# Modulation rows, the last squares and the attention unit's order in a two-layer hybrid block

## The chip, the cores and the metric

The kernel runs on one core of one Trainium2 chip. The metric is the device time of one execution in microseconds (us). Five engines work in parallel and wait for each other by semaphores: TensorE (PE) multiplies, VectorE (DVE) and ScalarE (ACT) do elementwise work, GpSimd (POOL) helps a little, SyncE (SP) issues the transfers.

## What is computed

Two layers on 128 context tokens and 512 latent tokens, 1024 wide. Layer 0 mixes with a pooling branch and a gated convolution, layer 1 with grouped attention; each has a gated feed-forward part, and a shift, scale and gate that come from a conditioning vector.

```python
def modulate(x, g, shift, scale):
    return rms_norm(x, g) * (1 + scale) + shift
...
        sh1, sc1, g1, sh2, sc2, g2 = ada_params(c, w_ada[l], b_ada[l])
        h = modulate(x, norm_g[l, 0], sh1, sc1)
        if l % 2 == 0:
            y = even_mixer(h, w_in_even[i], pool_w[i], pool_scale[i], conv_w[i], conv_b[i], w_out_even[i])
        else:
            q, k, v = qkv_proj(h, w_qkv[i], q_gain[i], k_gain[i])
...
            y = blocked_attention(q, k_all, v_all) @ w_o[i]
        x = x + g1 * y
        h = modulate(x, norm_g[l, 1], sh2, sc2)
        x = x + g2 * swiglu(h, w_ffn_in[l], w_ffn_out[l])
    y_sample = rms_norm(x, final_g)
```

## The kernel before

**Layout.** All 640 tokens lie along the free axis; features lie on the 128 partitions in 8 blocks. Each fp32 operand is split into a high part and a remainder (`pair`, L143: ACT copies, DVE subtracts), and each product is three matmuls, high by high, high by low and low by high (`block_mm`, L286). A weight block of 128 output features is 48 matmuls of about 148 ns, 7.1 us in all.

**Stages.** In the order of the trace: a startup written out by hand (to 53 us); the mixer's input projection "pi", 13 blocks besides the first three (to 155 us); its output projection "po" (to 212 us); the feed-forward part of layer 0, whose 22 hidden blocks are worked in three passes of 8, 8 and 6, each with a first product "fi" and a second product "fo" (to 655 us); the q, k and v projection "pq" and attention (to 870 us); the rest of attention's output projection "wb"; layer 1's feed-forward part; and the final norm. Most of "fi" (line L648) is a fast scheme in `fast_blocks` with seven half-size products per unit, p1 to p7.

**Order.** The program is traced once, in the order of the Python code. Outside the startup a list scheduler at compile time takes for every engine the ready instruction that was traced first, and it judges readiness by a model of its own. So the traced order is a priority and not the final order. After that each engine runs its queue strictly in order.

**Modulation rows.** The shift, scale and gate vectors of a layer have 48 blocks of 128 numbers. A "row" in this text is what gives one block: a weight tile of 128 x 1024, loaded by one transfer of 512 KB, multiplied by two conditioning vectors and summed on DVE (`AdaDve.run`, L362, multiply-and-sum at L377). In layer 0's mixer it takes two DVE instructions of 1024 columns; later, where the scratch tile is a PSUM bank of 512 columns, four. `ada.run(n)` puts n rows at a place in the traced order, and `self.load()` at its end asks for a later row. `PI_ROWS` (L39) gives the rows ahead of each "pi" block, L1081 those of "po", and `each` and `fast_each` (L1099, L1100) those of the feed-forward part: `each` by block of a second product, `fast_each` by unit n and product p of the fast scheme. `EARLY` (L37) rows must be done when "po" ends.

**Pooling.** `mixer_in` (L1044) gives the first four blocks to `pool_branch` (L936), which adds shifted copies on DVE (L949) and later scales and splits (`pool_mid`, L955) and multiplies by a small matrix (`pool_end`, L972). A block's result leaves PSUM in `scaled_main` (L536, instruction L538 on DVE) and `scaled` (L543 on ACT); the three PSUM tiles of two banks go round, so the third next tile needs this.

**Between "po" and "fi".** `updater` (L580) adds a block to x (L513, L527), squares it, prepares it for the next product (`prep`, L490 and L492) and, after the last block, copies the shift into two extra columns (`prep_shift`, L505 and L506), which the first "fi" block reads.

**Attention.** 34 units: one head by 128 queries, and two units for the context queries. `scores` multiplies q and k into PSUM tile 0; `peak` and `exps` are the softmax; `weights` normalises; `turn` transposes into PSUM tile 1; `keep` splits the result into a "pt" tile, of which there is one for each part (the pool has one buffer) and which holds two units; `values` multiplies by v and reads that tile; `store` splits the outcome. In the loop unit u's scores go with the turn of unit u-1 and, for every second unit, the values of unit u-2. `fills` are quarters or eighths of projection blocks ("pieces" of "pq" and "wa", 6 matmuls or 12), which give PE work between.

**The end.** The last two blocks of the last second product are done in two spans of 384 and 256 columns (`last1`, L1477). For each span the squares of all eight blocks are summed, on DVE for the last two (L447), and a matmul with a matrix of ones (L471, plain fp32, two passes) sums over partitions. Then come Ln, Exp and three DVE steps (L478 to L483), and the scaled output (L1491).

Of the kernel before, what the change touches and what calls it, by code (L numbers as in the profile page):

```python
# [11 lines left out]
AF = mybir.ActivationFunctionType  # L12
# [5 lines left out]
KB = D // P  # L18
# [17 lines left out]

EARLY = 28  # L37

PI_ROWS = (1, 1, 0, 0, 1, 1, 2, 1, 2, 2, 2, 1, 2)  # L39
WINDOWS = (2, 4, 8, 16)  # L40
PAD = 8
UL = PAD + CTX + PAD + LAT + PAD
# [20 lines left out]
def hybrid_step(  # L63
# [23 lines left out]
    V, S, G, PE = nc.vector, nc.scalar, nc.gpsimd, nc.tensor  # L87
# [8 lines left out]
    def ps_tile(name, at=None):  # L96

        if at is None:
            at = ps_turn[0] % ps_turn[1]
            ps_turn[0] += 1  # L100
        return psum.tile([P, 2, 512], F32, tag=f"mm{at}", bufs=1, name=name)
# [4 lines left out]
    def tmp(name):  # L106
        return tpool.tile([P, UL], F32, tag="t", name=name)

    x = pers.tile([P, KB, T], F32, name="x")
    bufA = (pers.tile([P, KB, TX], F32R, name="ah"), pers.tile([P, KB, TX], F32R, name="al"))  # L110
    bufB = (pers.tile([P, KB, TX], F32R, name="bh"), pers.tile([P, KB, TX], F32R, name="bl"))
    sm = pers.tile([P, NS], F32, name="sm")
    kc = pers.tile([P, NC], F32, name="kc")
    ones = pers.tile([P, P], F32, name="ones")
# [4 lines left out]
    rstd = pers.tile([P, T], F32, name="rstd")  # L119
# [70 lines left out]
    class Stream:  # L190
# [7 lines left out]
        eng = V  # L198
# [222 lines left out]
    class Norm:  # L421
# [24 lines left out]
            if k:  # L446
                (eng or G).tensor_tensor(out=self.acc[:, cols], in0=self.acc[:, cols], in1=sq[:, cols], op=ALU.add)  # L447

        def finish(self, span=None, spare=7, eng=None):
            rsqrt_of(self.acc, rstd, self.name, 1, span, spare, eng)  # L450

    def log_exp_tables():
        tc.keep_in_program_order(S.preload_act_table_set("natural_log_exp_and_others"))

    def rsqrt_of(acc, out, name, f, span=None, spare=None, eng=None):

        if span is None:
            a, b, cut = 0, T, halves  # L460
            ps = ps_tile(f"ms_{name}")
            ms = pmain(ps)
            to = [(ps[:, h, 0:HT], h * HT, h * HT + HT) for h in range(2)]
        else:
            a, b = span
            cut = lambda t: t
            ms = ps_small(f"ms_{name}_{a}")[:, 0 : b - a]
            to = [(ms, a, b)]
        if spare is None:
            for p, lo, hi in to:  # L470
                PE.matmul(p, ones, acc[:, lo:hi], start=True, stop=True)  # L471
        else:
            pair(bufB, acc[:, a:b], lambda t: t[:, spare, a:b], eng or V)
            for i in range(2):
                for p, lo, hi in to:
                    PE.matmul(p, onesr, bufB[i][:, spare, lo:hi], start=i == 0, stop=i == 1)
        y, ac = tmp(f"y_{name}_{a}")[:, a:b], acc[:, a:b]
        S.activation(cut(y), ms, AF.Ln, bias=epst, scale=float(f))  # L478
        S.activation(y, y, AF.Exp, scale=-0.5)
        S.activation(ac, y, AF.Square)  # L480
        V.scalar_tensor_tensor(out=cut(ac), in0=ms, scalar=EPS / f, in1=cut(ac), op0=ALU.add, op1=ALU.mult)
        V.tensor_scalar(ac, ac, -0.5 * f, 1.5, op0=ALU.mult, op1=ALU.add)
        V.tensor_tensor(out=out[:, a:b], in0=y, in1=ac, op=ALU.mult)  # L483
# [87 lines left out]
    def project(name, rhs, kn, n, done, ext=False, each=None, start=0):  # L571
        cut = HT if ext else CUT
        for i in range(start, n):
            ps = ps_tile(f"{name}_{i}")
            w = ws.next()
            if each:
                each(i)
            pipe.step(lambda: block_mm(ps, w, rhs, kn, ext=ext, cut=cut), lambda: done(i, ps))
# [192 lines left out]
    with tc.tile_pool(name="pool1", bufs=1) as p1:  # L771
# [6 lines left out]
        def ada_load(ch):  # L778
# [7 lines left out]
        ada = AdaDve(  # L786
            [(0, 4, 4)]
            + [(0, 8 * p, 8) for p in (2, 4, 3)]
            + [(0, 40 + b, 1) for b in range(8)]
            + [(1, 8 * p, 8) for p in (1, 0, 2, 4, 3)]  # L790
        )
# [28 lines left out]
        nrm = Norm("a0")  # L820
# [13 lines left out]
        acc = {ch: ada_acc(ch) for ch in (2, 3)}  # L834
# [38 lines left out]
        acc = ada_acc(0)  # L873
# [185 lines left out]
        for m in range(3):  # L1059
# [8 lines left out]
            ext=True,  # L1068
            each=lambda i: ada.run(PI_ROWS[i]),
        )  # L1070

        out_done = updater(0, 16, Norm("a1"), (bufA, 0, 1))
# [5 lines left out]
            pipe.step(lambda: block_mm(fps[m], fw[m], bufB, KB, ks=range(KB - 1), cut=CUT))  # L1078
        for m in range(2):
            pipe.step(lambda: block_mm(fps[m], fw[m], bufB, KB, ks=(KB - 1,), cut=CUT), lambda: out_done(m, fps[m]))  # L1080
        project("po", bufB, KB, KB, out_done, each=lambda i: ada.run(1), start=2)  # L1081

        assert ada.at == EARLY and not ada.raw
        early.close()
# [4 lines left out]
        with tc.tile_pool(name="pool4", bufs=1) as p4:  # L1089
            ada.home(p4, p1, 2, ps_small("junk"), silb)  # L1090
            ada.limit = len(ada.todo)
            ada.load()
            ada.load()
            more = tuple(p4.tile([P, 3 * 4 * HT], F32R, tag=t, name=t) for t in ("x0h", "x0l"))
            ffn(
                0,
                bufA,
                bufA,
                each=lambda i, gi, plain=False: ada.run(0 if plain else (1, 2, 1, 2, 2, 2, 2, 2)[i] if gi == 0 else (1, 2, 2, 2, 2, 2, 1, 0)[i]),  # L1099
                fast_each=lambda gi, n, p: ada.run(int(p == 6 and gi > 0)),  # L1100
                last=last0,
                spare=(tuple(t.rearrange("p a b -> p (a b)") for t in bufB), more),
            )
            assert ada.at == len(ada.todo)

    bufA, bufB = bufB, bufA


    with tc.tile_pool(name="pool2", bufs=1) as p2:
# [274 lines left out]
        units = []  # L1384
# [30 lines left out]
        with ExitStack():  # L1415
            for u, unit in enumerate(units):
                pipe.now += 1
                for f in posts:
                    f()
                posts = []  # L1420
                unit.scores()
                last = units[u - 2] if u > 1 and units[u - 2].values else None
                if last:
                    last.values()
                if u:
                    units[u - 1].turn()
                unit.peak()
                unit.exps()
                if u:
                    units[u - 1].keep()  # L1430
                unit.weights()
                spent += W_UNIT + (W_VALUES if last else 0)
                while fills and not posts and spent + W_PIECE / 2 <= work * (u + 1) / len(units):
                    posts = [f for f in (fills.pop(0)(),) if f]
                    spent += W_PIECE
                if last:
                    last.store()
                pipe.run_due()
# [24 lines left out]
        out_done = updater(1, 16, Norm("b1"), (bufA, 1, 1))  # L1463
# [13 lines left out]
    def last1(kn):  # L1477
        nrm = Norm("fin")

        def gain(k, cols=slice(0, T)):  # L1480
            S.activation(x[:, k, cols], x[:, k, cols], AF.Copy, scale=sm[:, S_FG + k : S_FG + k + 1])

        def whole(k, ps):
            residual(ps, k, 1, 40)
            nrm.add(k)
            gain(k)

        def out(ks, cols):
            n = cols.stop - cols.start
            xs = x[:, ks, cols]  # L1490
            V.tensor_tensor(  # L1491
                out=xs, in0=xs, in1=rstd[:, None, cols].broadcast_to((P, ks.stop - ks.start, n)), op=ALU.mult
            )
            nc.sync.dma_start(yT[:, ks, cols], xs)

        project("fo1_2", bufA, kn, KB - 2, whole)
        log_exp_tables()
        w = [ws.next(), ws.next()]
        ps = [ps_tile(f"fo1_2_{m}") for m in (KB - 2, KB - 1)]
        spans = ((0, 3 * P), (3 * P, T))  # L1500
        for h, (lo, hi) in enumerate(spans):
            cols = slice(lo, hi)
            for m in range(2):
                for k in range(kn):
                    for a, b in THREE:
                        PE.matmul(
                            ps[m][:, h, 0 : hi - lo],
                            w[m][a][:, k, :],
                            bufA[b][:, k, cols],
                            start=k == 0 and a == b,  # L1510
                            stop=k == kn - 1 and a == 1,
                        )
                parts = [(c, max(a, lo), min(b, hi)) for c, a, b in SEG if a < hi and b > lo]
                update(KB - 2 + m, 1, 40, [(c, a, b, ps[m][:, h, a - lo :]) for c, a, b in parts])
                nrm.add(KB - 2 + m, V, cols)
            with tc.high_priority():
                nrm.finish((lo, hi), None)
            for m in range(2):
                gain(KB - 2 + m, cols)
            if not h:  # L1520
                out(slice(0, 4), cols)
        for h, ks in ((0, slice(4, 8)), (1, slice(0, 4)), (1, slice(4, 8))):
            out(ks, slice(*spans[h]))

    whole_b = tuple(t.rearrange("p a b -> p (a b)") for t in bufB)
    more = tuple(p3.tile([P, 3 * 4 * HT], F32R, tag=t, name=t) for t in ("xh", "xl"))
# [11 lines left out]
        last=last1,  # L1538
        spare=(whole_b, more),
        each=lambda i, gi, plain=False: gates.run(0 if plain or gi else 1),  # L1540
# [114 lines left out]
```

## Time and profile before

| | before |
|---|---|
| median of 3 runs | 1357.52 us (1357.14 to 1358.26) |
| the profiled execution's own time | 1356.08 us |
| its span, first to last instruction | 1354.3 us |
| PE busy | 1326.0 us, 98% |
| DVE busy | 1068.6 us, 79% |
| ACT busy | 637.7 us, 47% |
| mean granted TensorE clock | 0.993 |

Busy time is the time in which an engine has an instruction in hand. PE and its weight loads overlap. A wait in the profile names the engine that waited and the instruction that released it. A window row gives for a stretch of time each engine's busy time and, in brackets, its instructions, then the granted TensorE clock as a share of full speed, the share of the DMA engines and the rate.

### The profile page before, as it was taken

How to read it: one execution, taken by the hardware profiler on the slowest of the kernel's cores; microseconds unless marked ns; L12 is line 12 of the kernel's file. 1: busy time of each engine (PE TensorE's matmuls, PEld its weight loads, DVE VectorE, ACT ScalarE, POOL GpSimd, SP SyncE). 2: the span in 40 equal slices, each digit the busy share in tenths (PEclk: the TensorE clock that was granted, in tenths of full speed). 3: DMA queues.
4: the chain of work that ended last, by engine and by line, in shares of the span. 5: the costliest groups of instructions: out<-in, count | busy, mean ns of one | idle time of the engine just before them, and what ended most of it. 6: DMA issues, size and time to landing. Idle time of an engine off the chain costs nothing.

```text
span 1354.3 us, 22409 instructions
## 1 busy us (share of the span) xinstructions
PE 1326.0 (98%) x8952; PEld 1295.1 (96%) x8952; DVE 1068.6 (79%) x2025; ACT 637.7 (47%) x1159; POOL 46.3 (3%) x56
## 2 busy tenths in 40 slices
PE   8999999999999999999999999999999999999996
PEld 6899999999999999999998999999999999999995
DVE  4899897978999999899877677589876777446744
ACT  5433246753145522454666675477541355314543
POOL 0000000000000000000022221000000000000001
PEclk9999999999999999999999999999999999999998
DMA  9735522125543454334331110131134022311212
GB/s 365 286 125 171 171 94 94 63 67 176 179 141 109 146 187 151 120 137 164 133 101 48 48 48 32 51 137 60 38 137 171 32 94 76 112 63 63 78 47 78
DMA packets 36807, 155.53 MB, mean 115 GB/s; under 512 B 3936, under 2 KB 11104, under 8 KB 25952
## 3 DMA queue, kind: packets, MB, share of 16 engines
q1 hardware_dynamic: 36704, 154.12, 33.0%
q8 instruction: 70, 1.15, 0.4%
q14 instruction: 33, 0.27, 0.1%
HBM read 148.60 MB, written 2.88 MB: 112 GB/s over the span
## 4 chain that ended last, share of the span: by engine, by line
PE 82%; DVE 12%; ACT 3%; issue 2%; DMA 1%; SPq 0%; POOL 0%; DVEq 0%; ACTq 0%; POOLq 0%
PE fi L648 28%; PE fo L294 18%; PE fi L294 8%; PE pi L294 6%; PE pq L294 5%; PE po L294 4%; DVE junk L377 4%; PE wb L294 2%; PE wa L294 2%; PE o L1371 2%; PE s L1321 2%; DVE wl_fi_p L147 1%; PE t L1354 1%; DMA rawa<-wada 1%; DMA x<-xT 1%
## 5 line engine op out<-in xcount | busy, mean ns | idle before, releaser
L146 ACT ACTIVATE wh_fi_p<-raw_fi 128x512 fp32r<-128x512 f32 x252 | 154.5, 627 | 226.0 <-PE fi L648 122.3
L377 DVE CUSTOM_DVE_ANT_0 junk<-rawa,silb 128x512 f32<-128x512 f32 (+1 forms) x280 | 224.0, 800 | 7.9 <-DMA rawa<-wada 3.5
L147 DVE TENSOR_TENSOR wl_fi_p<-raw_fi,wh_fi_p 128x512 fp32r<-128x512 f32 x252 | 171.3, 687 | 65.6 <-ACT wh_fi_p L146 65.3
L146 ACT ACTIVATE wh_fo<-raw_fo 128x1024 fp32r<-128x1024 f32 (+1 forms) x48 | 47.5, 990 | 147.8 <-PE fo L294 129.5
L648 PE MATMUL fi<-bh,wl_fi_p 128*128 128x320 f32 x288 | 89.0, 309 | 0.0
L648 PE MATMUL fi<-bh,wh_fi_p 128*128 128x320 f32 x288 | 88.8, 308 | 0.0
L648 PE MATMUL fi<-ah,wl_fi_p 128*128 128x320 f32 x288 | 88.7, 308 | 0.0
L648 PE MATMUL fi<-al,wh_fi_p 128*128 128x320 f32 x288 | 88.7, 308 | 0.0
L648 PE MATMUL fi<-ah,wh_fi_p 128*128 128x320 f32 x288 | 88.4, 307 | 0.0
L648 PE MATMUL fi<-bl,wh_fi_p 128*128 128x320 f32 x288 | 88.4, 307 | 0.0
L294 PE MATMUL fo<-al,wh_fo 128*128 128x384 f32 (+1 forms) x352 | 81.0, 311 | 0.0
L294 PE MATMUL fo<-ah,wh_fo 128*128 128x384 f32 x352 | 80.8, 311 | 0.1
L294 PE MATMUL fo<-ah,wl_fo 128*128 128x384 f32 x352 | 80.5, 310 | 0.0
L294 PE MATMUL fo<-bh,wh_fo 128*128 128x384 f32 x328 | 75.2, 310 | 0.0
L294 PE MATMUL fo<-bh,wl_fo 128*128 128x384 f32 (+1 forms) x328 | 75.1, 310 | 0.0
L294 PE MATMUL fo<-bl,wh_fo 128*128 128x384 f32 x328 | 75.0, 310 | 0.0
L513 DVE SCALAR_TENSOR_TENSOR x<-fo,mod,x 128x128 f32<-128x128 f32 (+1 forms) x52 | 18.5, 359 | 70.7 <-PE fo L294 67.2
L648 PE MATMUL fi<-x0h,wh_fi_p 128*128 128x320 f32 x216 | 68.1, 319 | 0.5
L648 PE MATMUL fi<-xh,wh_fi_p 128*128 128x320 f32 x216 | 67.9, 320 | 0.5 <-ACT fi L660 0.4
L648 PE MATMUL fi<-xl,wh_fi_p 128*128 128x320 f32 x216 | 66.5, 309 | 0.0
L648 PE MATMUL fi<-xh,wl_fi_p 128*128 128x320 f32 x216 | 66.5, 309 | 0.0
L648 PE MATMUL fi<-x0h,wl_fi_p 128*128 128x320 f32 x216 | 66.4, 308 | 0.0
(376 smaller groups left out, 3774.7 us busy)
## 6 DMA issues: line engine op xcount, KB each, us to landing
raw_fi<-wfi SPq DMA_DIRECT2D x44, 1024.0 KB, 4.8
rawa<-wada SPq DMA_DIRECT2D x84, 512.0 KB, 3.4
raw_fo<-wfo SPq DMA_DIRECT2D x16, 1024.0 KB, 4.9
raw_ada<-wada SPq DMA_DIRECT2D x12, 512.0 KB, 7.3
raw_in<-win SPq DMA_DIRECT2D x6, 1024.0 KB, 5.2
raw_fo<-wfo SPq DMA_DIRECT2D x8, 768.0 KB, 4.3
raw_qkv<-wqkv SPq DMA_DIRECT2D x6, 1024.0 KB, 5.5
raw_out<-wout SPq DMA_DIRECT2D x4, 1024.0 KB, 5.9
```

Source lines behind the costliest of these rows:

```text
L146: S.activation(h, src, AF.Copy)
L147: eng.tensor_tensor(out=l, in0=src, in1=h.bitcast(F32), op=ALU.subtract)
L294: PE.matmul(ps[:, h, 0 : hi - lo], w[a][:, k, cols], rhs[b][:, k0 + k, lo:hi], start=k == 0 and a == b, stop=k == kn - 1 and a == 1,)
L377: op = V.tensor_tensor_reduce(out=self.junk, in0=raw[:, cols], in1=self.silb[:, c, cols], scale=1.0, scalar=0.0, op0=ALU.mult, op1=ALU.add ...
L513: V.scalar_tensor_tensor(out=xs, in0=got[:, 0 : b - a], scalar=mod[l][:, gate0 + m, c : c + 1], in1=xs, op0=ALU.mult, op1=ALU.add,)
L648: PE.matmul(out, w[a][:, k, :], ops.get(OPERAND[p], b)[:, k, :], start=fresh and k == 0 and a == b, stop=k == ops.kn - 1 and a == 1, skip_ ...
L1321: PE.matmul(self.ps[:, hf, 0:HT], bufB[a][:, self.h, q0 : q0 + P], kt[b][:, self.kv, hf * HT : hf * HT + HT], start=n == 0, stop=n == 2,)
L1354: PE.transpose(flat(pt)[:, s * P : s * P + P], self.pe[:, s * P : s * P + P], ident)
L1371: PE.matmul(po[:, 0 : 2 * P], vt[a][:, self.kv, s * P : s * P + P], got[b][:, s, :], start=s == 0 and n == 0, stop=s == 4 and n == 2,)
```

## The change

Four edits. (1) Modulation rows: in "pi" 14 rows in place of 16, none ahead of its first four blocks; the two others go to "po", ahead of blocks 3 and 5. (2) In layer 0's feed-forward part the first pass's second product has the row counts of the second pass's, 12 rows in place of 14 and one and none at its last two blocks; the two others go to the first pass's fast units 1 and 2, at product p6. (3) In the final norm the squares of the very last block are no longer added to the sum on DVE; they go as a second operand into the matmul with ones, which accumulates over both. (4) In attention's loop turn, keep and values come behind the pieces in the traced order, and values behind turn and keep.

```diff
-PI_ROWS = (1, 1, 0, 0, 1, 1, 2, 1, 2, 2, 2, 1, 2)
+PI_ROWS = (0, 0, 0, 0, 1, 2, 1, 2, 1, 2, 1, 2, 2)
...
-                PE.matmul(p, ones, acc[:, lo:hi], start=True, stop=True)
+                PE.matmul(p, ones, acc[:, lo:hi], start=True, stop=more is None)
+                if more is not None:
+                    PE.matmul(p, ones, more[:, lo:hi], start=False, stop=True)
...
-        project("po", bufB, KB, KB, out_done, each=lambda i: ada.run(1), start=2)
+        project("po", bufB, KB, KB, out_done, each=lambda i: ada.run(1 + (i in (3, 5))), start=2)
...
-                each=lambda i, gi, plain=False: ada.run(0 if plain else (1, 2, 1, 2, 2, 2, 2, 2)[i] if gi == 0 else (1, 2, 2, 2, 2, 2, 1, 0)[i]),
-                fast_each=lambda gi, n, p: ada.run(int(p == 6 and gi > 0)),
+                each=lambda i, gi, plain=False: ada.run(0 if plain else (1, 2, 2, 2, 2, 2, 1, 0)[i]),
+                fast_each=lambda gi, n, p: ada.run(int(p == 6 and (gi > 0 or n in (1, 2)))),
...
                 unit.scores()
                 last = units[u - 2] if u > 1 and units[u - 2].values else None
-                if last:
-                    last.values()
-                if u:
-                    units[u - 1].turn()
                 unit.peak()
                 unit.exps()
-                if u:
-                    units[u - 1].keep()
-                unit.weights()
                 spent += W_UNIT + (W_VALUES if last else 0)
                 while fills and not posts and spent + W_PIECE / 2 <= work * (u + 1) / len(units):
                     posts = [f for f in (fills.pop(0)(),) if f]
                     spent += W_PIECE
+                if u:
+                    units[u - 1].turn()
+                    units[u - 1].keep()
+                if last:
+                    last.values()
+                unit.weights()
                 if last:
                     last.store()
...
-                nrm.add(KB - 2 + m, V, cols)
+                if m:
+                    sq = tmp(f"sq_last_{h}")
+                    S.activation(sq[:, cols], x[:, KB - 1, cols], AF.Square)
+                else:
+                    nrm.add(KB - 2, V, cols)
             with tc.high_priority():
-                nrm.finish((lo, hi), None)
+                nrm.finish((lo, hi), None, more=sq)
```

More of the change, by code (lines that the diff above doesn't have):

```diff
@@ L447, in add, with finish, rsqrt_of @@
                 (eng or G).tensor_tensor(out=self.acc[:, cols], in0=self.acc[:, cols], in1=sq[:, cols], op=ALU.add)
-        def finish(self, span=None, spare=7, eng=None):
-            rsqrt_of(self.acc, rstd, self.name, 1, span, spare, eng)
+        def finish(self, span=None, spare=7, eng=None, more=None):
+            rsqrt_of(self.acc, rstd, self.name, 1, span, spare, eng, more)
     def log_exp_tables():
         tc.keep_in_program_order(S.preload_act_table_set("natural_log_exp_and_others"))
-    def rsqrt_of(acc, out, name, f, span=None, spare=None, eng=None):
+    def rsqrt_of(acc, out, name, f, span=None, spare=None, eng=None, more=None):
         if span is None:
```

## Prediction

> **What bounds the kernel now.** I read first the busy time by stage, then PE's waits, then the places of the longest waits in order of time.
>
> ```profile
> 53.00:155.00 102.00, 99.87 (x667) 99.26 (x665) 97.91 (x157) 36.66 (x62) 1.00 (x18) 0.98 0.48 163
> 155.00:212.00 57.00, 57.00 (x389) 57.00 (x388) 47.89 (x81) 20.86 (x32) 0.00 (x0) 1.00 0.35 126
> 270.00:317.00 47.00, 46.98 (x317) 46.06 (x317) 34.94 (x55) 24.79 (x48) 0.00 (x0) 1.00 0.27 90
> 317.00:382.00 65.00, 63.73 (x431) 63.49 (x430) 62.61 (x162) 12.23 (x18) 0.00 (x0) 1.00 0.51 170
> 480.00:537.00 57.00, 56.92 (x385) 56.66 (x384) 53.08 (x129) 9.54 (x13) 0.00 (x0) 1.00 0.53 182
> 710.00:870.00 160.00, 154.82 (x1116) 149.07 (x1117) 114.36 (x251) 101.38 (x212) 29.08 (x15) 1.00 0.14 44
> 1339.00:1355.00 16.00, 2.66 (x15) 1.73 (x14) 9.29 (x13) 3.77 (x10) 0.00 (x0) 0.62 0.47 164
> ```
>
> After a stretch and its length, the columns are PE, weight loads, DVE, ACT, POOL, then the granted clock. PE is the bound nearly everywhere: 57.00 of 57 in "po", 46.98 of 47 in "fi". So DVE work that moves is worth only what PE waits for it, and work on PE's own path counts in full. PE has free time in four of these rows: 2.1 us in "pi" (102.00 - 99.87), 1.3 us in the first "fo" (65.00 - 63.73), 5.2 us in attention, and the end. In the first two DVE is nearly full (97.91 of 102, 62.61 of 65). Who ended the waits:
>
> ```profile
> PE ms_fin L471 <- DVE ssq_fin L447: 2.2, 1, 2.2
> PE pi L294 <- ACT ev L543: 2.1, 1, 2.1
> PE fi L642 <- DVE x L527: 1.3, 1, 1.3
> PE t L1354 <- DVE pt_0l L147: 1.3, 3, 0.6
> PE o L1371 <- DVE pt_0l L147: 1.2, 2, 0.7
> PE t L1354 <- DVE pt_2l L147: 1.0, 1, 1.0
> PE t L1354 <- ACT pe L1240: 0.7, 1, 0.7
> PE o L1371 <- ACT pt_0h L146: 0.6, 3, 0.2
> ```
>
> Each edit aims at one of these: one wait in "pi", one ahead of "fi", the attention's five rows (4.8 us together), one at the end. The startup's waits lie ahead of all edits and stay.
>
> **Part 1a, rows out of the pooling blocks.** The wait in "pi" and what follows it:
>
> ```profile
> 78.11 0.81 DVE L538 TENSOR_TENSOR ev<-pi,rstd 128x640 f32<-128x640 f32 x1
> 79.24 0.56 PE L294 MATMUL pi<-ah,wh_in 128*128 128x320 f32 x2 [2.13 <-ACT ev L543]
> L377 DVE CUSTOM_DVE_ANT_0 junk<-rawa,silb 128x1024 f32<-128x1024 f32 x6 | 7.3, 1212 | 0.0
> 79.24 8.91 PE pi L294 x48
> 89.02 7.15 PE pi L294 x48
> 79.96:83.37 3.41, 3.41 (x15) 3.41 (x15) 3.41 (x8) 0.78 (x2) 0.00 (x0) 0.50 0.23 91
> 376.40:380.30 3.90, 2.63 (x19) 2.39 (x18) 3.83 (x13) 1.15 (x2) 0.00 (x0) 1.00 0.38 111
> ```
>
> PE needs a PSUM tile whose evacuation (L538, then L543 on ACT) stands in DVE's queue at 78.11, behind pooling and modulation. The third row groups the multiply-and-sums between 53 and 88 us: six, of which the two removed rows are four. They take DVE 4 x 1.21 = 4.8 us ahead of that evacuation, and none of the other work there waits for PE. So L538 starts near 73.3; PE followed it by 79.24 - 78.11 = 1.13, so it could go on at 74.4. It is free only at 79.24 - 2.13 = 77.1. The wait goes with 2.7 us to spare. Late next is nothing that I can find: the running count of rows in "pi" is below the old one at every block.
>
> The wait has a tail. The block behind it took 8.91 us, the next one 7.15: 1.76 us more, because the clock was granted at 0.50 for 3.41 us. The later wait of 1.3 us, last row, left it at 1.00. So the edit is worth 2.13 + 1.76 = 3.9 us. Bounds: 2.1 if the half clock comes anyway, 3.9 if not; I take 3.9, since the half clock follows at once upon this wait.
>
> [...]
>
> **Part 1b, the same rows into "po".**
>
> ```profile
> 162.10:169.20 7.10, 7.10 (x50) 7.10 (x49) 1.52 (x4) 1.14 (x2) 0.00 (x0) 1.00 0.23 74
> 169.20:204.50 35.30, 35.30 (x242) 35.30 (x241) 34.91 (x58) 14.91 (x24) 0.00 (x0) 1.00 0.25 90
> 204.50:211.60 7.10, 7.10 (x51) 7.10 (x50) 4.14 (x9) 2.66 (x5) 0.00 (x0) 1.00 0.86 295
> 208.69 0.17 DVE L506 TENSOR_TENSOR al<-mod,ah 128x16 fp32r<-128x16 f32 x1
> 211.55 0.45 PE L294 MATMUL fi<-ah,wh_fi 128*128 128x320 f32 x2
> 211.84 0.45 PE L294 MATMUL fi<-al,wh_fi 128*128 128x320 f32 x2
> 211.75 0.35 DVE L513 SCALAR_TENSOR_TENSOR x<-po,mod,x 128x128 f32<-128x128 f32 x1 [2.89 <-PE po L294]
> ```
>
> Here DVE is full: 34.91 of 35.30 us from block 2 to block 6. Two more rows are 4 x 1.22 = 4.9 us. The free time at 162 to 169 us (7.10 - 1.52) lies ahead of them and did not serve the rows of block 2 either. So DVE comes out of block 6 late by 4.9 - 0.4 = 4.5 us, and the last block has 7.10 - 4.14 = 3.0 to spare. Residuals and weight splits stand that (three PSUM tiles, weights a block ahead). The shift copies do not: the last row gives the last numbers of the shift, and "fi" reads them in its first matmuls. L506 would end at 208.69 + 0.17 + 4.5 = 213.4, where PE wants it at 211.84: 1.5 us. Bounds: 0 if the copies go ahead of the 4.1 us of other DVE work of that block (they are two instructions of 0.17), 1.5 + 1.76 = 3.3 if the wait brings the half clock too (1.3 us did not, 2.1 did). I take 1.0, nearer to the row without half clock.
>
> **Part 2, rows off the end of the first "fo".**
>
> ```profile
> L377 DVE CUSTOM_DVE_ANT_0 junk<-rawa,silb 128x512 f32<-128x512 f32 x55 | 38.2, 695 | 1.9 <-DMA rawa<-wada 1.0
> ```
>
> Modulation takes 38.2 of DVE's 62.61 us in that stage. With three rows less at the last two blocks (4 x 0.70 us each) the last residual, L527, is no longer behind them. The second pass's "fo" already has exactly these counts, and there PE has 56.92 of 57.00 us. So the 1.3 us go. The two rows that arrive in "fi" cost 2 x 4 x 0.70 = 5.6 us of DVE, which has 47.00 - 34.94 = 12.1 free. Their loads, on SP's queue, come earlier, not later. Value 1.3, between 0 (something else holds the tile) and 1.3.
>
> **Part 3, attention's order.**
>
> ```profile
> 819.43 1.78 PE wa L294 x12
> 821.22 0.90 PE s L1321 x6
> L146 ACT ACTIVATE pt_2h<-t x16: 686/704/708, 729.0 to 871.4; 128x640 fp32r<-128x640 f32 x16
> L147 DVE TENSOR_TENSOR pt_2l<-t,pt_2h x16: 808/818/826, 729.7 to 872.1; 128x640 fp32r<-128x640 f32 x16
> ```
>
> No instruction is added. PE's waits are for the softmax or for keep (0.70 + 0.82 = 1.52 us): transposes and values came to the head of the queue too early. With pieces (0.89 us for 6 matmuls, 1.78 for 12) between the scores and both of them, values get the cover of a turn more, and a turn gets a piece after its softmax. I count as gone the values' waits, 1.2 + 0.6, and the one for the softmax, 0.7: 2.5 us. The turn's waits for the free PSUM tile (1.3 + 1.0) I leave. Bounds: 4.8 (all) and, below nothing, the third rival.
>
> **Part 4, the end.**
>
> ```profile
> 1336.24 0.53 ACT L445 ACTIVATE sq_fin<-x 128x384 f32<-128x384 f32 x1 [1.95 <-DVE x L513]
> 1336.80 0.56 DVE L447 TENSOR_TENSOR ssq_fin<-ssq_fin,sq_fin 128x384 f32<-128x384 f32 x1 [0.59 <-ACT sq_fin L445]
> 1337.51 0.88 PE L471 MATMUL ms_fin<-ssq_fin,ones 128*128 128x384 f32 x2
> 1337.93 0.58 PE L1506 MATMUL fo<-bh,wh_fo 128*128 128x256 f32 x1
> 1342.38 0.34 DVE ssq_fin L447
> ```
>
> The add goes from the first span's chain: 1337.51 - (1336.24 + 0.53) = 0.74 us. In the second span it goes from DVE's queue, where the chain has 0.34 for it. Each matmul with ones has a second pair of passes; in the first span that pushes PE's last product by 1337.93 - 1337.51 = 0.42 us, and all of the second span with it. The first operand's passes can run while the last block is still updated. Sum 0.74 + 0.34 - 0.42 = 0.7; bounds 1.1 (the passes hidden) and -0.4 (only they count). I take 0.6.
>
> **Sum.** -3.9 + 1.0 - 1.3 - 2.5 - 0.6 = -7.3 us. The profiled span goes from 1354.3 to 1347.0, that execution's own time from 1356.08 to 1348.8. It lay 1.4 us under the median of 1357.52, on which the forecast is set: 1350.2. A measurement here can tell about 0.2%, 2.7 us.
>
> **Rivals.**
>
> *Attention moves nothing.* The scheduler takes what is ready in its own model, and already put pieces between; the new priorities may leave the waits as they are. Sum -4.8: 1352.7.
>
> *The shift copies fall behind the last residual.* They are traced behind the last block's update and preparation. If the late last row makes them wait there, they come after another 4.14 us of such work from 211.75 on: PE waits for some 4.2 us, and the half clock adds 1.76, 5.9 in place of 1.0. Sum -2.4: 1355.1. Against it: in the trace they ran before that update.
>
> *Slower: the single "pt" buffer.* The new order traces keep ahead of the values that free its buffer. So for 16 pairs keep starts only after values, and the next turn needs keep done. Where only the scores lie between, 0.90 us against 1.52, PE waits 0.62 each, and behind the waiting keep stands, on ACT and DVE, the next softmax: 16 x 0.62 = 9.9 us in place of a gain of 2.5. Sum +5.1: 1362.6. It decides where less than a piece of 0.89 us lies between; against it, there are about two pieces per unit and the scheduler sees the buffer.
>
> *The half clock stays*, because it has another cause than the wait. The gain in "pi" is the wait of 2.1 alone: sum -5.5, 1352.0. The row that speaks against it is the 0.50 right behind the wait, and 1.00 in all later stage rows but the last. [...]
>
> *All waits go*: -3.9 - 1.3 - 4.8 - 1.1 and nothing in "po": -11.1: 1346.4.
>
> **How the numbers follow.** Forecast 0.45, attention nothing 0.17, half clock stays 0.07, all waits go 0.08: these are faster by over 0.2%, 0.77 together. The shift copies, 0.13, end within 0.2%. The "pt" buffer, 0.10, is slower. The range leaves out the last of the fast cases and the slower one: 1347.0 to 1355.5.
>
> **What would show it.** Right: no PE wait near 77 us, no granted clock of 0.5 between the startup and the end, no wait for L527 ahead of the second pass's "fi", fewer than 3 us free on PE in attention. A wait for L505 or L506 at the start of the first "fi" tells the price of part 1b. Wrong: a wait in "pi" that only changed its place, turns that wait for "pt" in every second unit, or PE's last product over 0.5 us later than the other terms explain.

## The result, and the profile after

The changed kernel takes 1364.84 us (median, 1364.13 to 1365.85), against 1357.58 us for the kernel before on the same chip. The ratio is 1.0055, with a 95% interval of 1.0045 to 1.0065: slower by 7.3 us, where 7.3 us less was forecast. The profiled execution of after took 1364.13 us with a span of 1362.3, 8.0 us over the span of before. (Line numbers from L492 on are those of before plus two: L506 is now L508, L513 is L515, L527 is L529.)

Busy time by stretch, first the kernel before, then after. Each stretch begins with the first matmul of its stage, so the lengths are stage lengths: the first pass up to "fo", from there to the second pass's "fo", attention, and from the last second product to the end. After has two rows more in front, "pi" without its first block and "po".

```profile
211.50:319.50 108.00, 107.98 (x728) 107.06 (x727) 87.97 (x141) 68.28 (x124) 0.00 (x0) 1.00 0.20 69
319.50:479.10 159.60, 158.02 (x1060) 155.38 (x1059) 151.21 (x340) 60.86 (x112) 0.00 (x0) 1.00 0.45 152
709.90:868.00 158.10, 152.92 (x1104) 147.17 (x1105) 112.36 (x247) 100.36 (x212) 29.18 (x15) 1.00 0.14 44
1297.00:1354.30 57.30, 44.66 (x293) 43.25 (x292) 25.71 (x41) 23.18 (x34) 7.86 (x5) 0.90 0.16 58
```

```profile
55.50:152.50 97.00, 97.00 (x653) 96.77 (x653) 93.59 (x147) 36.42 (x61) 1.01 (x18) 1.00 0.49 168
152.50:209.20 56.70, 56.70 (x387) 56.70 (x386) 49.94 (x84) 20.61 (x32) 0.00 (x0) 1.00 0.30 103
209.20:320.50 111.30, 108.78 (x729) 107.13 (x728) 94.49 (x167) 68.41 (x124) 0.00 (x0) 1.00 0.28 96
320.50:478.70 158.20, 157.89 (x1059) 155.34 (x1059) 146.51 (x320) 60.83 (x112) 0.00 (x0) 1.00 0.43 147
709.50:876.10 166.60, 153.57 (x1104) 147.65 (x1105) 112.79 (x247) 101.82 (x210) 29.37 (x15) 1.00 0.13 42
1305.10:1362.30 57.20, 45.79 (x297) 43.78 (x296) 24.73 (x39) 23.55 (x34) 7.86 (x5) 0.93 0.16 58
```

The reader sees where the time is: attention has the same 1104 matmuls and takes 8.5 us more, and nearly all of it is PE without work, 166.60 - 153.57 = 13.0 us against 158.10 - 152.92 = 5.2. "pi" is full now, at full clock. The first "fi" costs 3.3 us more, the stage behind it 1.3 less (1.58 us of free PE became 0.31), the end 0.1 less.

For "pi" the evacuations in the two traces say the rest (columns: count, shortest, median and longest ns, then first and last start):

```profile
L538 DVE TENSOR_TENSOR ev<-pi,rstd x16: 811/819/826, 50.9 to 155.6; 128x640 f32<-128x640 f32 x16
```

```profile
L540 DVE TENSOR_TENSOR ev<-pi,rstd x16: 814/820/826, 52.4 to 153.4; 128x640 f32<-128x640 f32 x16
```

The startup ended 1.5 us later (52.4 - 50.9), and "po" still began 2.4 earlier (154.9 before, 152.5 after), so "pi" gained 3.9. The startup's 1.5 us belong to no edit: its half clock lasted 6.8 us in this trace and 3.4 in the trace of before, and of the later runs, whose code up to there is that of after, a1 starts L540 at 50.5 us and b1 at 52.3 (a7 has no half clock there at all). Together: 1.5 - 3.9 + 3.3 - 1.3 + 8.5 - 0.1 = 8.0 us.

PE's waits in after (engine and line, what released it, then us in total, times, longest):

```profile
PE wa L294 <- DVE x L529: 4.1, 5, 1.2
PE o L1373 <- ACT pt_0h L146: 2.5, 3, 0.9
...
PE fi L294 <- DVE al L508: 1.4, 1, 1.4
PE o L1373 <- ACT pt_2h L146: 1.4, 1, 1.4
PE o L1373 <- DVE qsq L1214: 1.1, 1, 1.1
PE pq L294 <- ACT q L1186: 1.0, 1, 1.0
PE fi L294 <- ACT ah L492: 1.0, 1, 1.0
```

The waits of before in "pi", for L527 and of the transposes "t" for "pt" are gone. In their place stand waits of the values "o", and two waits that before did not have at all: the pieces "wa" and "pq" wait until their own PSUM tile is emptied.

### The profile page after: what moved, and what is told of

It is laid out like the page before. It is cut to its first block, busy times and chain, and to the rows that moved or that the text cites. A ratio compares the mean times of both kernels' runs of the same rounds, so it can differ in the third digit from the quotient of the medians.

```text
span 1362.3 us, 22409 instructions
## 1 busy us (share of the span) xinstructions
PE 1328.5 (98%) x8956; PEld 1296.0 (95%) x8956; DVE 1067.9 (78%) x2023; ACT 640.5 (47%) x1159; POOL 46.5 (3%) x56
## 4 chain that ended last, share of the span: by engine, by line
PE 84%; DVE 9%; ACT 4%; issue 2%; DMA 1%; SPq 0%; POOL 0%; DVEq 0%; ACTq 0%; POOLq 0%
PE fi L650 27%; PE fo L294 22%; PE fi L294 8%; PE pi L294 8%; PE pq L294 5%; PE po L294 4%; PE wb L294 2%; PE s L1323 1%; PE wa L294 1%; PE o L1373 1%; DVE wl_fi_p L147 1%; DVE junk L377 1%; PE t L1356 1%; ACT wh_fi_p L146 1%; DMA x<-xT 1%
## 5 line engine op out<-in xcount | busy, mean ns | idle before, releaser
L515 DVE SCALAR_TENSOR_TENSOR x<-fo,mod,x 128x128 f32<-128x128 f32 (+1 forms) x52 | 18.5, 359 | 76.0 <-PE fo L294 69.7
```

What stands on the lines that cost most here:

```text
L515: V.scalar_tensor_tensor(out=xs, in0=got[:, 0 : b - a], scalar=mod[l][:, gate0 + m, c : c + 1], in1=xs, op0=ALU.mult, op1=ALU.add,)
```

## The experiments

Two theories of attention's loss stood at the start. **Cover**: turn and values need other matmuls between themselves and what they wait for, and the new order takes these away. **pt**: with values behind turn and keep, the one "pt" buffer is freed too late, and keep, on ACT and DVE, waits and holds up what stands behind it. All kernels are changes of after unless said otherwise; "stage" is attention from its first scores to "wb", 158.1 us before and 166.6 after.

**Attention or the rest.** a1 is after with the loop of before; a2 is before with the new loop. Their diff is the loop of the change, undone and done.

> The changed kernel with attention's loop in the order of before; the other three edits stay. If the loss is attention's alone, it goes: 1364.8 - 8.3 = 1356.5 us, PE free time between 710 and 870 us back from 13.0 to about 5, and the start of the first fi still waits 2.4 us. If part of the loss comes from the moved rows through later stages, it stays above 1358.

> The kernel before with the new attention loop alone. If the four edits add up, 1357.6 + 8.3 = 1365.9 us. If the new loop is slow only after the moved rows, near 1357.6.

a1 took 1355.33 us, ratio 0.9989 (0.9979 to 0.9998), stage 158.5. a2 took 1366.83 us, ratio 1.0062 (1.0045 to 1.0080), stage 169.1, with 12.7 us of free PE, the same five waits of "wa" (4.1 us), and two half clocks of 3.4 us. The loop alone makes the change slow, and the rest of it is worth only about 1.5 us.

**The order's two parts.** a3, a4 and a5 take the old loop of a1 and move calls:

```
a3: scores, turn, values, softmax, keep, weights, pieces
a4: scores, values, softmax, pieces, turn, keep, weights
a5: scores, turn, softmax, keep, weights, pieces, values
```

> As the first, but turn ahead of values; keep, weights and the pieces stay in their old places, the pieces last. Theory cover (pieces spent ahead of the turn leave keep and the evacuation of the pieces' own PSUM tile bare): within 1 us of the first, about 1356.5. Theory pt (keep ahead of the values that free its single buffer): most of the loss is here, 1361 to 1365.

> As the first, but turn and keep behind the pieces; values stay directly behind the scores, so the pt buffer is free in time. Theory cover: most of the loss is here, 1360 to 1364, with pieces waiting for the residual's L529. Theory pt: none of it, about 1356.5.

> As the first, but values behind the pieces; scores, turn, softmax, keep, weights, pieces, values. Theory cover: keep lies under the pieces as before, so within 1 us of the first, or up to 2 us faster since values no longer wait for pt. Theory pt: keep waits for values that now come last, so as slow as the change or slower, 1364 or more.

a3 took 1361.22 us, ratio 1.0034 (1.0024 to 1.0044), stage 165.2; a4 1367.20, ratio 1.0077 (1.0057 to 1.0097), stage 169.5; a5 1361.34, ratio 1.0036 (1.0021 to 1.0051), stage 164.9. Neither theory has all three: cover had a3 and a5 near a1, pt had a4 near it. Each of them loses 6 us or more of stage, and the parts do not add up to the whole. Part of a4's loss, and of a3's, is the half clock: 6.8 us of it behind a wait of 2.4 us in a4, 3.4 us in a3, which is some 3.4 and 1.7 us of time (an estimate from before, where 3.41 us of it made a block 1.76 us longer).

**What empties the pieces' tile.** The longest row of the waits is "wa" for x. a7 takes away that work: `residual(ps, m, 1, 16)` for "wa" becomes nothing, so the first four heads' share is left out of the residual. c1 keeps it and only calls it earlier in the loop:

```diff
                     spent += W_PIECE
+                pipe.now += 1
+                for f in posts:
+                    f()
+                pipe.now -= 1
+                posts = []
                 if u:
                     units[u - 1].turn()
```

> The changed kernel without the update of x by the wa blocks, which leaves the first four heads out of the residual; PSUM tile 2 then has no reader in that part, and DVE about 1.1 us less work per block. Theory cover: the five waits of wa for L529, 4.1 us, go, and nothing else: about 1360. If those waits only stand for another delay, other waits take their place and the time stays within 1 us of 1364.

> The changed kernel with one edit: what follows a finished piece (the residual, or q's first evacuation) is called right behind the pieces and ahead of turn, keep and weights, no longer at the head of the next unit. Theory 'tile 2': since pieces now stand ahead of keep and weights while what empties their PSUM tile is still called at the next unit's head, this work has fallen behind keep (1.5 us) and weights on DVE and ACT. Then PE's waits of wa for x (4.1 us) and of pq for q (1.1) go, the stage from the first scores to the next stage falls from 166.6 to 161 to 163 us, and the kernel to 1359 to 1361. Rival 'pt': the one buffer of the turned weights, with values called behind the next keep, makes the loop longer; the waits of wa change into waits of t or o for pt, stage 165 to 167, kernel 1363 to 1365. Rival 'cover': turn, keep and values come straight after one another whatever else moves; the waits of o for pt_0h stay or grow, stage 164 to 167.

a7 took 1360.74 us (one run): the waits of "wa" are gone and the stage is 161.2 us, but the next stage takes 35.5 in place of 31.1, since 25 matmuls of the first now run in it. From the first scores to "fi" that is 196.7, after has 197.7, before 189.2. The waits did not move on: PE's free time over the two stages falls from 13.0 to 9.9 us. But a7 has a half clock of 3.4 us at 800.7, which after does not have and which takes 1.7 back. The time of the whole kernel says less, because a7 also has no half clock in the startup (mean granted clock 0.996, after 0.995). c1 took 1364.66 us, ratio 1.0049 (1.0032 to 1.0066), its stage 168.1 us with a half clock of 3.4 at 802.5, and its waits are those of after to 0.1 us. In the two traces PE, DVE and ACT run the same instructions of attention in the same order: the scheduler places the call as it did before, so c1 decides nothing between the theories.

The timeline of after shows what stands ahead of the residual. Two units in the second half, without most rows of PE and ACT; columns are start, length, engine, line and tiles, with idle time and releaser in brackets:

```profile
825.44 0.28 PE L1373 MATMUL o<-pt_2h,vtl 128*128 128x256 f32 x1
...
825.82 0.71 ACT L146 ACTIVATE pt_0h<-t 128x640 fp32r<-128x640 f32 x1 [1.30 <-PE o L1373]
826.56 0.82 DVE L147 TENSOR_TENSOR pt_0l<-t,pt_0h 128x640 fp32r<-128x640 f32 x1 [1.25 <-ACT pt_0h L146]
827.30 0.41 DVE L147 TENSOR_TENSOR al<-o,ah 128x256 fp32r<-128x256 f32 x1
827.63 0.81 DVE L1333 TENSOR_REDUCE mx<-s 128x1 f32<-128x640 f32 x1
828.42 0.35 DVE L515 SCALAR_TENSOR_TENSOR x<-wa,mod,x 128x128 f32<-128x128 f32 x1
828.81 0.74 DVE L529 SCALAR_TENSOR_TENSOR x<-wa,mod,x 128x512 f32<-128x512 f32 x1
829.69 0.53 PE L294 MATMUL wa<-ah,wh_wo 128*128 128x384 f32 x2 [0.77 <-DVE x L529]
```

Read it from top to bottom. ACT's keep is released by the last matmul of the values: its input, the transposes, was there 1.9 us earlier (they ended at 823.96), but the tile "pt" was not free. DVE stands idle behind it for 1.25 us. Then its queue runs keep's second half, the store of the values, the next unit's maximum, and only then the residual that empties the pieces' tile. PE waits for that. The row of waits names x, but what is late is "pt".

**Two buffers.** c2 gives "pt" two buffers (`bufs=2`); to make room, `tpool` has seven temporaries in place of eight. c3 has the seven alone.

> The changed kernel with two buffers for the turned weights (pt) in place of one; to make room, one of eight temporaries is gone. To be read against the next kernel, which has the seven temporaries alone. Theory 'pt' (keep waits for the values that free the one buffer): attention's stage is shorter than with one buffer by 5 us or more, near 158 to 161. Theories 'tile 2' and 'cover': within 1.5 us of the next kernel's stage, the waits of wa for x still about 4.

> The changed kernel with seven temporaries in place of eight and one pt buffer: the control of the kernel before it. Every theory: attention's stage within 2 us of the changed kernel's 166.6; any difference elsewhere is the price of the eighth temporary.

One run each: c2 1364.03 us, stage 166.9; c3 1363.11, stage 166.2. By the totals pt fails. But c2 has a half clock of its own in the first half (units 10 to 13), behind a wait of 2.15 us:

```profile
762.60:769.40 6.80, 5.89 (x25) 5.49 (x26) 3.70 (x8) 2.72 (x6) 0.00 (x0) 0.50 0.01 2
```

and its waits of "wa" for x are down to one of 0.6 us. So the lag was followed unit by unit. The table gives how far each unit's scores start behind a1's (us, both from their first scores); from unit 23 on the pieces are those of "wa". The last three lines are of kernels that come next.

```
unit      9     14     16     19     23     25     27     29     31    end
after  +0.0   +1.7   +3.7   +4.0   +4.6   +5.5   +6.4   +7.3   +7.8   +8.1
c2      0.0   +5.2   +7.2   +8.2   +9.0   +9.0   +9.0   +9.0   +9.0   +8.4
d1     -0.1   -0.1   -0.1    0.0   +0.1   +0.1   +0.9   +1.8   +2.1   +2.5
d2     -0.1    0.0    0.0   -0.2   -0.1   -0.1   -0.1   -0.1   -0.1   -0.4
d3      0.0   +1.7   +3.7   +4.0   +4.6   +5.5   +5.5   +5.5   +5.5   +5.4
```

After loses in both halves. c2 loses nothing from unit 23 on. Up to there it has lost 9.0 us, of which the half clock is some 3.4 (half of its 6.8, by the same estimate); the other 5.6 are no less than after's 4.6, so in the first half the second buffer brought nothing.

**The halves apart.** d1 has the old loop's calls up to unit 22 (the first branch) and the new ones behind it (the second); d2 is d1 with c2's two "pt" buffers and seven temporaries; d3 is d1's mirror.

```diff
+                if u < 23:
...
+                else:
...
```

> The changed kernel with the old loop for units 0 to 22 and the new one from unit 23 on, where the pieces are those of wa. Theory 'pt' (keep waits for the values that free the single pt buffer, and the residual that empties the pieces' PSUM tile stands behind keep on DVE): the lag against the old loop is about 0 up to unit 23 and grows by 0.8 to 0.9 us per two units from there: stage 158.5 + 3 to 4 = 161.5 to 162.5 us, waits of wa for x 3 to 4 us, kernel 1358 to 1360. Rival 'first half': the waits of the second half are carried over from a bad start; stage within 1 us of 158.5, kernel 1355 to 1356.

> As the kernel before it, with two pt buffers and seven temporaries in place of eight. Theory 'pt': stage 158 to 159.5, waits of wa for x under 1 us, kernel 1355 to 1357. Rival 'pieces' (the place of the pieces ahead of turn and keep is itself the cause): stage as with one buffer, 161.5 to 162.5.

> The mirror: the new loop for units 0 to 22 (pieces of pq), the old one from 23 on. If the two halves lose independently: stage 158.5 + 4 to 5.5 = 162.5 to 164 us, lag reached by unit 23 and constant from there, kernel 1359 to 1361. If the second half inherits: the lag goes on growing to 7 or 8, stage 166.

d1 took 1357.66 us, ratio 1.0005 (0.9996 to 1.0014), stage 161.0, a little less lost than "pt" expected. d2 took 1356.47, ratio 0.9997 (0.9988 to 1.0006), stage 158.1. PE's waits from 800 to 871 us, first d1, then d2, each with the only row over the view's threshold:

```profile
PE wa L294 <- DVE x L529: 2.7, 3, 1.2
```

```profile
PE s L1323 <- ACT pe L1340: 0.6, 1, 0.6
```

In both, PE runs nearly the same sequence there (scores, twelve matmuls of "wa", transposes, and the values behind every second unit's transposes); with one buffer, some of the next twelve stand ahead of the scores, and these are the ones that wait. Seven temporaries alone change nothing in this order: c3's is that of after. With the second buffer the waits of "wa" are gone and the stage is that of a1. So in the second half the single buffer is the whole cause. The gaps agree: in after PE's wait of "wa" for x came back five times (0.65, three times 0.77, and 1.18 us), and in d2 it went with the buffer.

d3 took 1361.41 us, ratio 1.0035 (1.0021 to 1.0048), stage 164.0. It loses 5.4 us, all of it by unit 25, and then stays level. d1's 2.5 and d3's 5.4 make 7.9 of after's 8.1: the halves lose independently.

**The first half.** The rows behind one turn of a first-half unit, before and after, PE alone:

```profile
721.61 0.71 PE L1354 MATMUL t<-kc,pe 128*128 128x128 f32 x5
722.07 0.54 PE L294 MATMUL pq<-bl,wh_qkv 128*128 128x320 f32 x2
722.45 0.45 PE L294 MATMUL pq<-bh,wl_qkv 128*128 128x320 f32 x2
723.11 0.38 PE L1371 MATMUL o<-pt_0h,vth 128*128 128x256 f32 x1 [0.21 <-ACT pt_0h L146]
```

```profile
721.71 0.71 PE L1356 MATMUL t<-kc,pe 128*128 128x128 f32 x5
723.31 0.38 PE L1373 MATMUL o<-pt_0h,vth 128*128 128x256 f32 x1 [0.90 <-ACT pt_0h L146]
```

Before, four matmuls of "pq" stood between the transposes and the values that read them. After, none: the pieces were spent ahead of the turn, and the values wait 0.90 in place of 0.21 us. d5 is d3 with one piece of each unit held back and put between keep and values:

```diff
-while fills and not posts and spent + W_PIECE / 2 <= work * (u + 1) / len(units):
+while fills and not posts and spent + 3 * W_PIECE / 2 <= work * (u + 1) / len(units):
...
                         units[u - 1].keep()
+                    while fills and not posts and spent + W_PIECE / 2 <= work * (u + 1) / len(units):
+                        posts = [f for f in (fills.pop(0)(),) if f]
+                        spent += W_PIECE
                     if last:
                         last.values()
```

> The kernel with the new loop in units 0 to 22, with one of each unit's pieces held back from its place ahead of the transposes and put between keep and the values. Theory 'cover' (values bare behind their transposes): the waits of o for pt fall from 5.3 to 2 or 3 us, the stage from 163.95 to 160 to 162, kernel 1357 to 1359.5. Rival 'order': values must come ahead of the transposes, as in the old loop, and the piece only moves the wait to the transposes or the scores; stage 163 to 165.5, kernel 1360.5 to 1363.

d5 took 1357.66 us, ratio 1.0009 (1.0000 to 1.0019), stage 161.4: 2.6 of the 5.4 us came back, inside what cover expected for the stage. PE's waits in the stage, first d3, then d5:

```profile
PE o L1373 <- ACT pt_0h L146: 2.5, 3, 0.9
PE o L1373 <- DVE pt_0l L147: 1.4, 3, 0.5
PE o L1373 <- ACT pt_2h L146: 1.4, 1, 1.4
PE o L1373 <- DVE qsq L1214: 1.1, 1, 1.1
PE pq L294 <- ACT q L1186: 1.0, 1, 1.0
```

```profile
PE o L1373 <- ACT pt_0h L146: 2.6, 3, 0.9
PE o L1373 <- DVE pt_0l L147: 0.9, 2, 0.5
...
PE o L1373 <- DVE pt_2l L147: 0.7, 1, 0.7
...
PE o L1373 <- ACT pt_2h L146: 0.2, 1, 0.2
```

But not in the way expected. The values' waits for "pt" fell only from 5.3 to 4.4 us, not to 2 or 3; the two last rows of d3, 2.1 us together, went. They lie around the context unit, where d3's lag rises from 0.3 to 3.7 us (units 13 to 16) and d5's only from 0 to 1.2. So the place of the pieces is part of the first half's cost. The other 2.9 us stay open. The swap alone (a3) also loses in this half, 4.0 us of it at unit 15, but some 1.7 of these are its half clock. a5 has none, and it keeps the pieces between the turn and the values; it only lets the values follow the turn, and by unit 23 it is 3.0 us behind a1. So the order of turn and values seems to cost about what d5 left; through which wait is not shown.

**Better versions.** b1 takes a1 and gives the two rows moved out of "pi"'s early blocks to its late ones, none of them to "po":

```diff
-PI_ROWS = (0, 0, 0, 0, 1, 2, 1, 2, 1, 2, 1, 2, 2)
+PI_ROWS = (0, 0, 0, 0, 1, 2, 2, 2, 1, 2, 2, 2, 2)
...
-        project("po", bufB, KB, KB, out_done, each=lambda i: ada.run(1 + (i in (3, 5))), start=2)
+        project("po", bufB, KB, KB, out_done, each=lambda i: ada.run(1), start=2)
```

c4 is b1 with keep called ahead of the softmax. d4 is b1 with part 4 undone, the squares of the last block added on DVE again.

> The old attention loop, and the two rows that went to po put into later blocks of pi (blocks 6 and 10), so that po has its old rows. The wait of 2.4 us at the start of the first fi goes, 3.2 us with its tail, and the one in pi does not come back: 3 us under the kernel with the old attention loop, 1353 to 1354. If DVE in pi has no room there, PE waits again in pi and the gain is under 1 us.

> The best kernel so far (old attention order, rows late in the pooling blocks, 1352.1) with keep called ahead of the softmax in place of behind it, so that the order is scores, values, turn, keep, softmax, weights, pieces. Theory 'cover' (the waits left in the old order are for keep, 4.5 us of 5.3): the waits of t and o for pt_0l and pt_0h fall by 1 to 3 us and the waits of t for pe rise by less; stage 155.5 to 158, kernel 1349.5 to 1352. Rival 'softmax first': PE's next turn waits for the softmax that now stands behind keep's 1.5 us, stage 160 to 166, kernel 1354 to 1360.

> The best version so far (1352.1) with the end of the kernel as it was before the change: last squares added on DVE, one pair of matmuls with ones. As the traces of before and after have it, the new end is worth 0.1 us: from the start of the last product's stage to the end 57.3 in place of 57.2 us, kernel 1351.5 to 1353. As the prediction had it, it is worth 0.6: 57.8 and 1352 to 1353.5. If the second pass with ones costs more than the chain that it shortens, the time falls by 0.2 to 0.5.

b1 took 1352.11 us, ratio 0.9956 (0.9941 to 0.9971), and beats both kernels. From the first "fi" to the first "fo" it needs 108.1 us, as before, and "pi" keeps its gain. c4 took 1353.13, ratio 0.9970 (0.9960 to 0.9981): its stage is 159.9 against b1's 158.2, and 1.4 of the 1.7 us come between units 21 and 23. Neither theory had that; keep ahead of the softmax helps nothing. d4 took 1352.78, ratio 0.9968 (0.9955 to 0.9980); from the last second product to the end its trace has 57.3 us (1291.4 to 1348.7), b1's 57.2 (1293.3 to 1350.5). Part 4 is worth 0.1 us, which no total here can tell.

## Why the prediction failed

**Part 1a** (-3.9 forecast, -3.9 measured): right. The wait is gone, and the half clock with it. a2, which has the old rows, has both (a wait of 2.1 us, then a clock of 0.50 from 81.4 us for 3.4); in after, a1, a3, a4, a5, d1, d2, d3 and d5, which have the new rows, the granted clock is 1.00 from 79.96 to 83.37 us, so the rival in which it stays is out.

**Part 1b** (+1.0 forecast, +3.3 measured): what came is the rival in which the shift copies fall behind the last residual. This is the trace of after:

```profile
209.17 0.45 PE L294 MATMUL fi<-ah,wh_fi 128*128 128x320 f32 x2
209.37 0.35 DVE L515 SCALAR_TENSOR_TENSOR x<-po,mod,x 128x128 f32<-128x128 f32 x1
209.64 0.17 DVE L399 TENSOR_TENSOR mod<-got,sm 128x16 f32<-128x16 f32 x1
209.72 0.74 DVE L529 SCALAR_TENSOR_TENSOR x<-po,mod,x 128x512 f32<-128x512 f32 x1
...
210.61 0.81 PE L294 MATMUL fi<-ah,wh_fi 128*128 128x320 f32 x2 [0.99 <-ACT ah L492]
...
213.38 0.17 DVE L508 TENSOR_TENSOR al<-mod,ah 128x16 fp32r<-128x16 f32 x1
...
213.61 0.42 PE L294 MATMUL fi<-al,wh_fi 128*128 128x322 f32 x1 [1.45 <-DVE al L508]
```

L399 completes the last row, and the copies need it. In before it ran at 205.59, 6.0 us ahead of the first "fi" matmul; here it runs 0.5 us behind that matmul, between the two parts of the last block's residual (L515 and L529). L508 then stands behind this residual, its preparation, a weight split and a sum of squares. The failed step is that the delay of 4.5 us moves the copies and leaves their place in the queue as it was: counted from the first "fi" matmul, L506 ended 2.7 us ahead of it in before, and L508 ends 4.4 us behind it, 7.1 us later. That the text has 213.4 for an end at 213.55 is luck, since PE came to "fi" at 209.17 and not at 211.55. The rival's price was too high: PE waits 0.99 and 1.45 us, 2.4 together in place of 4.2, and the half clock did not come in after. The other 0.8 us of the 3.3 are busy time of PE (108.78 against 107.98 us) and were not followed further.

Nor is it PE's earlier arrival that turns DVE's work into a wait. b1 has the same gain in "pi", the old rows in "po" and no such wait; its L508 ends 2.7 us ahead of the first "fi" matmul, as in before:

```profile
206.28 0.17 DVE L508 TENSOR_TENSOR al<-mod,ah 128x16 fp32r<-128x16 f32 x1
...
209.13 0.45 PE L294 MATMUL fi<-ah,wh_fi 128*128 128x320 f32 x2
```

So it is the two rows in "po" that cost the 3.3 us, and late in "pi" there was a free place for them. In a1 the half clock followed upon the same waits of 0.99 and 1.45 us, and its stage took 112.8 us, 4.8 more than before:

```profile
212.20:215.60 3.40, 3.40 (x15) 3.40 (x14) 1.47 (x3) 0.37 (x2) 0.00 (x0) 0.50 0.65 270
```

**Part 2** (-1.3 forecast, -1.3 measured): right.

**Part 3** (-2.5 forecast, +8.5 measured): the sign was wrong. The step that failed is "values get the cover of a turn more, and a turn gets a piece after its softmax". The turn did get its cover: its waits went from 3.0 us to 0.1. The values lost theirs, and their waits rose from 1.9 to 6.2 us, because the pieces that had stood between transposes and values were spent ahead of both; d3 puts 5.4 us on the first half's order, and d5 2.6 of them on the place of the pieces. And "No instruction is added" left out that the order decides how long the one "pt" tile is held.

The slower rival named that tile, and its total of 1362.6 us is close to the 1364.84 measured, but it is only a third of the story: d1 and d2 give the buffer 2.5 to 2.9 us, in the second half only. Its working put the loss on the turns and on the softmax behind keep; measured, the turns hardly wait, and the work behind the waiting keep that PE misses is the residual for the pieces' tile. Its "there are about two pieces per unit", said against it, was the wrong reading: it is just these pieces that wait.

**Part 4** (-0.6 forecast, -0.1 measured): the sum's smallest term was mis-sized. The timeline of after:

```profile
1345.26 0.53 ACT L1518 ACTIVATE sq_last<-x 128x384 f32<-128x384 f32 x1 [2.86 <-DVE x L515]
...
1345.84 0.91 PE L473 MATMUL ms_fin<-sq_last,ones 128*128 128x384 f32 x2
1346.30 0.57 PE L1507 MATMUL fo<-bl,wh_fo 128*128 128x256 f32 x1
```

The step from square to matmul is 1345.84 - (1345.26 + 0.53) = 0.05 us, where before had 0.74. But relative to the stage's start the square itself begins 0.9 us later (1345.26 - 1305.1 = 40.2, before 1336.24 - 1297.0 = 39.2), so the gain was spent ahead of it: 0.7 gained on one link, 0.9 lost on the one before. Of these 0.9 the pass over the first operand, which PE now runs ahead of the last block, is 0.46 (it starts at 1342.47, the next product at 1342.93); the text had counted 0.42 for that and nothing more. Where the other 0.4 went is not settled. In the second span the matmul comes only 0.06 us after the square (before 0.80), but this could bring nothing:

```profile
1350.70 3.43 DVE L1492 TENSOR_TENSOR x<-x,rstd 128x1536 f32<-128x1536 f32 x2
...
1354.05 0.42 DVE L483 SCALAR_TENSOR_TENSOR ssq_fin<-ms_fin,ssq_fin 128x256 f32<-128x256 f32 x1
```

DVE is busy with the first span's output until 1354.1 and only then takes up the second span's norm, for which ACT was ready at 1352.8. In before it is the same, from 1342.63 to 1346.0. This output starts 45.6 us after the stage's start in after and 45.7 in before, and the end follows it.

## What to carry to other kernels

Where a loop has one buffer between a producer and a consumer, an order that puts the producer's next turn ahead of the consumer makes the producer's engines wait, and the wait shows up under the name of whatever stands behind it in their queues (here ACT waited 1.30 us and DVE 1.25 for "pt", and PE 0.77 under the name of x): look at who released the first idle instruction, not at the row of waits. Before moving filler work, note what it covers now; moved ahead of one wait, it leaves another bare. And where rows are added to a full queue, ask what they fall behind and what passes them, and not only how late they make the rest: here the copies that PE needed lost their place to the last residual.

## What the runs showed of the hardware

The length of a wait alone does not decide on the half clock here. The granted clock was 0.50 behind a wait of 2.13 us in before (from 79.96 us, for 3.41 us), the waits of 0.99 and 1.45 us in a1 (from 212.2, for 3.4), the wait of 2.15 us in c2 (from 762.6, for 6.8) and that of 2.40 us in a4 (for 6.8). It stayed at 1.00 behind 1.27 us in before (from 376.4 to 384.0 us) and behind 0.99 and 1.45 us in after (from 211.0 to 216.0), the same waits as in a1. So it did behind the waits of 1.42 and 0.48 us in attention of after (from 798.03 to 805.0); in c1, whose waits are those of after to 0.1 us, it was 0.50 for 3.4 us at 802.5. Why the same waits went both ways is open.

The granted clock changed at 42.41, 45.82, 79.96, 83.37 and 1342.89 us in before, and at 40.27, 47.09 and 1354.40 in after. The stretches between are 3.41, 34.13, 3.41 and 1259.52 us, and 6.83 and 1307.31: 1, 10, 1 and 369, and 2 and 383 times 3.413, which is a tenth of the 34.13. Whether the place of a wait on these steps plays a part is not shown. Two half clocks of 6.8 us have PE without work inside them (0.91 of 6.80 us in c2, 0.78 of 6.82 in the startup of after); the two of 3.4 in before and the one in a1 have none (3.41 of 3.41 busy, and 3.40 of 3.40).

Each microsecond at half clock cost about half of one: the block of "pi" took 8.91 in place of 7.15 us with 3.41 us of it. By that measure, an estimate, the wait of 2.13 us in before cost 3.9 (2.13 + 1.76), and the one of 2.15 us in c2 some 5.5 (2.15 + half of 6.8).
